# State-space mixer with heads on partitions: scan, broadcast loads and grouped matmul bursts in a two-layer decoder trunk

## The chip, the cores and the metric

The kernel runs on one core of a Trainium2 chip. The metric is device time in microseconds (us) of one execution. A profiled execution adds a trace of five engines: TensorE (PE, whose weight loads are listed as PEld), VectorE (DVE), ScalarE (ACT), GpSimd (POOL) and SyncE (SP), which issues the DMAs.

## The reference

The program is a decoder trunk of two layers on 256 positions of width 1024. Each layer normalises its input, runs three token mixers side by side (a state-space mixer, a retention, a gated linear attention), adds the gated sum back, and then runs a gated MLP with a short convolution over positions. The change lies in the state-space mixer alone. With `xs` (8 heads of 64), `bm` and `cm` (2 groups of 64 states, four heads to a group) and one raw step per head and position, it computes

```python
dt = softplus(dt_raw + ssm_dt_bias)            # (256, 8)
a = -exp(ssm_a_log)                            # (8,)
cum = cumsum(dt * a)                           # over positions, per head
decay[t, s] = exp(cum[t] - cum[s])             # s <= t, else 0
y[t] = sum over s <= t of (cm[t] . bm[s]) * decay[t, s] * (dt[s] * xs[s])
y = y + ssm_d * xs                             # then gated by silu(z) and group-normed
```

The sum is written in chunks in the reference; both kernels take all 256 positions at once, as two blocks of 128.

## The kernel before

All large products are float32 products in three terms: a weight is loaded in pieces of 128 x 1024 (`piece`, line 167), ACT rounds it to a high part `whi` (line 183), DVE takes the rest `wlo` (line 184), and PE multiplies high by high, high by low and low by high (lines 227 to 229 with 256 columns, lines 274 to 276 with 512). There are four buffers for raw pieces and six for split ones; each request for a piece issues the loads of up to five pieces ahead.

`stream` runs the main line of these products for one layer after the other. At each `yield` of the main line, every side task whose count has run out is advanced once (lines 1086 to 1090). One such step is one pass over a slice of a weight: six matmuls of 512 columns in `tok_major`, twelve of 256 in `chan_major`. The side task of the change is `ssm` (line 567): its `yield W[i]` puts so many steps between two of its parts. So the emission order is written out by hand, and from it the framework's planner lays down the order of each engine at build time, by its own estimates of when an instruction is ready. After that every engine runs in order.

In each layer `ssm` is spawned after `take_small` (line 923), which leaves the raw steps of the 8 heads on partitions 0 to 7 and, for a second part of the same product, on 64 to 71. Beside it the main line runs z, the first gates, rq, rk and rv; before the retention (`ret`) is spawned, `ssm` is finished (line 962). Its parts before the change are these.

- Lines 570 to 585: PE turns the raw steps to positions on partitions (`pick` adds the two parts), and DVE and ACT compute `dt` (softplus, through `log1p`) and `da` on tiles of 128 x 16.
- Lines 586 to 592: eight PE transposes bring `xs` to positions on partitions.
- Lines 593 to 599: three PE products with a triangle of ones and a block of ones make the running sum `ncum`.
- Lines 600 to 605: POOL makes `val = dt * xs` and scales `xs` by `ssm_d`.
- Lines 607 to 612: PE turns `ncum` back to heads on partitions, and it is split into two parts in `cum`.
- `decay` (line 615), four times, for two heads each: PE spreads a head's row of `cum` over 128 partitions (line 620), ACT adds the other position's sum (lines 624 and 626), POOL masks the upper triangle (line 629), ACT takes the exponential (line 631). The tiles have the tag `st` with two buffers.
- `score` (line 634), once for each group of states: products over 64 partitions, 0 to 63 for one group and 64 to 127 for the other. `masked` (line 641) multiplies scores into a decay tile on DVE.
- `scan_out` (line 548), four times: 12 products of scores with values, 24 rows in the trace.
- Lines 664 to 678: the sum is gated and normed, and `branch_operand` (line 534) transposes it on PE.

PSUM tiles of these parts come from a ring of four (`mx_tile`). The retention after it uses the same `scan_out`, and in its own `score` (lines 723 to 729) two heads on partitions 0 to 63 and 64 to 127 follow each other.

## Time and profile before

| | us |
|---|---|
| median of 3 runs | 927.43 (927.09 to 927.57) |
| the profiled execution | 928.57 |
| its span in the trace | 926.8 |

Engines' busy times, the waits of an engine and the matmul rows are read from that one execution. The start of a row is exact; matmuls overlap, so the time that a matmul takes from the engine is the distance from its start to the next one's start, not the length of its row.

### The profile page before, as it was taken

To read this page: it belongs to the slowest core of one execution; us is meant where nothing else is said; L and a number is where in the kernel's file an instruction comes from. 1 tells how busy PE (TensorE), PEld (TensorE's weight loads), DVE (VectorE), ACT (ScalarE), POOL (GpSimd) and SP (SyncE) were. 2 spreads that over 40 slices of the span, in tenths; PEclk is the share of its full clock that TensorE was granted. 3 is DMA by queue.
4 is the path that set the end of the run, shared out by engine and by line. 5 is a ranking of instruction groups with operands and counts; after the bars stand their busy time and mean duration, and the time that the engine had idled before them with its cause. 6 is when DMAs were issued, how large, how long until landed. Compare 5 with 4: busy or idle time off the path is not lost.

```text
span 926.8 us, 15382 instructions
## 1 busy us (share of the span) xinstructions
PE 908.8 (98%) x5918; PEld 805.8 (87%) x5918; DVE 711.5 (77%) x1111; ACT 506.2 (55%) x748; POOL 78.4 (8%) x74
## 2 busy tenths in 40 slices
PE   8999999999999999999999999999999999999995
PEld 7779888888889999999898897888888999999994
DVE  6976888576768887778799578877657797787775
ACT  6665454454456555555566645544445575555552
POOL 3022200003200000000002131000220000000001
PEclk9999999999999999999999999999999999999998
DMA  8774666456665655565456656544666565555631
GB/s 255 261 252 153 224 191 174 155 163 210 197 182 161 203 183 185 185 191 191 148 174 190 201 174 220 160 155 146 209 204 202 160 199 187 184 182 187 184 107 45
DMA packets 51289, 169.95 MB, mean 183 GB/s; under 512 B 5968, under 2 KB 8336, under 8 KB 51088
## 3 DMA queue, kind: packets, MB, share of 16 engines
q1 hardware_dynamic: 50928, 168.46, 57.3%
q8 instruction: 46, 0.75, 0.3%
q10 hardware_dynamic: 288, 0.52, 0.2%
q14 instruction: 27, 0.22, 0.1%
HBM read 165.81 MB, written 1.05 MB: 180 GB/s over the span
## 4 chain that ended last, share of the span: by engine, by line
PE 87%; DVE 4%; issue 3%; DMA 3%; ACT 2%; SPq 1%; POOL 0%; ACTq 0%; POOLq 0%; DVEq 0%
PE mm L227 12%; PE mm L228 12%; PE mm L229 12%; PE mm L274 11%; PE mm L276 11%; PE mm L275 11%; PE mx L1025 4%; PE mx L1026 4%; PE mx L1027 4%; DMA raw<-w_all 2%; DVE wlo L184 1%; PE mx L558 1%; PE mx L542 1%; SPq L704 1%; DMA x_t<-x_t 1%
## 5 line engine op out<-in xcount | busy, mean ns | idle before, releaser
L184 DVE TENSOR_TENSOR wlo<-raw,whi 128x1024 fp32r<-128x1024 f32 (+1 forms) x300 | 376.5, 1257 | 126.2 <-ACT whi L183 123.4
L183 ACT CAST whi<-raw 128x1024 fp32r<-128x1024 f32 (+1 forms) x302 | 311.6, 1034 | 270.0 <-PE mm L276 111.8
L227 PE MATMUL mm<-slot_h,whi 128*128 128x256 f32 x992 | 282.0, 285 | 1.6 <-ACT slot_h L302 1.6
L228 PE MATMUL mm<-slot_l,whi 128*128 128x256 f32 x992 | 281.0, 283 | 0.4 <-DVE slot_l L303 0.2
L229 PE MATMUL mm<-slot_h,wlo 128*128 128x256 f32 x992 | 281.0, 283 | 0.0
L274 PE MATMUL mm<-whi,slot_h 128*128 128x512 f32 x512 | 204.3, 399 | 0.9 <-DVE tm L459 0.9
L275 PE MATMUL mm<-wlo,slot_h 128*128 128x512 f32 x512 | 200.3, 391 | 0.3 <-DVE wlo L184 0.3
L276 PE MATMUL mm<-whi,slot_l 128*128 128x512 f32 x512 | 200.3, 391 | 0.0
L227 PEld LDWEIGHTS mm<-slot_h,whi 128*128 128x128 f32 x992 | 189.8, 191 | 4.9 <-ACT slot_h L302 2.2
L228 PEld LDWEIGHTS mm<-slot_l,whi 128*128 128x128 f32 x992 | 189.9, 192 | 2.8 <-DVE slot_l L303 1.0
L229 PEld LDWEIGHTS mm<-slot_h,wlo 128*128 128x128 f32 x992 | 189.9, 191 | 0.4 <-DVE wlo L184 0.2
L274 PEld LDWEIGHTS mm<-whi,slot_h 128*128 128x128 f32 x512 | 96.2, 188 | 22.1 <-DVE tm L459 1.4
L276 PEld LDWEIGHTS mm<-whi,slot_l 128*128 128x128 f32 x512 | 96.2, 188 | 20.2
L275 PEld LDWEIGHTS mm<-wlo,slot_h 128*128 128x128 f32 x512 | 96.3, 188 | 19.2 <-DVE wlo L184 0.7
L1015 DVE SCALAR_TENSOR_TENSOR tm<-tm,par 128x255 f32<-128x255 f32 (+1 forms) x176 | 73.6, 480 | 0.7 <-ACT tm L1013 0.7
L1025 PE MATMUL mx<-whi,slot_h 128*128 128x512 f32 x176 | 69.1, 392 | 0.0
L1026 PE MATMUL mx<-wlo,slot_h 128*128 128x512 f32 x176 | 69.0, 392 | 0.0
L1027 PE MATMUL mx<-whi,slot_l 128*128 128x512 f32 x176 | 68.5, 389 | 0.0
L1013 ACT ACTIVATE tm<-tm,par 128x256 f32<-128x256 f32 x88 | 48.0, 593 | 4.3 <-DVE tm L1008 4.3
L1008 DVE TENSOR_TENSOR tm<-mm,r_bc 128x512 f32<-128x512 f32 x44 | 30.4, 691 | 23.0 <-PE mm L229 23.0
L1019 ACT CAST slot_h<-tm 128x256 fp32r<-128x256 f32 x44 | 17.9, 406 | 49.1 <-DVE tm L1018 49.1
L1027 PEld LDWEIGHTS mx<-whi,slot_l 128*128 128x128 f32 x176 | 33.1, 188 | 7.2
(189 smaller groups left out, 727.7 us busy)
## 6 DMA issues: line engine op xcount, KB each, us to landing
raw<-w_all SPq DMA_DIRECT2D x292, 512.0 KB, 3.6
gate_b<-gate_b SPq DMA_DIRECT2D x12, 256.0 KB, 3.5
st<-ret_decay SPq DMA_DIRECT2D x8, 384.0 KB, 4.2
raw<-w_all SPq DMA_DIRECT2D x10, 256.0 KB, 4.1
x_t<-x_t SPq DMA_DIRECT2D x4, 256.0 KB, 5.7
xt<-x_tok SPq DMA_DIRECT2D x1, 1024.0 KB, 5.7
r_c<-q SPq DMA_DIRECT2D x16, 64.0 KB, 2.0
r_d<-q SPq DMA_DIRECT2D x16, 64.0 KB, 2.0
```

The costliest lines, as they stand in the source:

```text
L183: nc.scalar.copy(h_out, r_in)
L184: nc.vector.tensor_tensor(l_out, r_in, h_out.bitcast(F32), ALU.subtract)
L227: nc.tensor.matmul(o, lhsT=wh[:, c], rhs=ah[:, k, :], start=first, stop=False)
L228: nc.tensor.matmul(o, lhsT=wh[:, c], rhs=al[:, k, :], start=False, stop=False)
L229: nc.tensor.matmul(o, lhsT=wl[:, c], rhs=ah[:, k, :], start=False, stop=last)
L274: nc.tensor.matmul(acc[t], lhsT=ah[:, k, c], rhs=wh, start=first, stop=False)
L275: nc.tensor.matmul(acc[t], lhsT=ah[:, k, c], rhs=wl, start=False, stop=False)
L276: nc.tensor.matmul(acc[t], lhsT=al[:, k, c], rhs=wh, start=False, stop=last)
L1015: nc.vector.scalar_tensor_tensor(a[:, d:], u[:, :T - d], mx.pc("fconv_w", 3 * ct + 2 - d), a[:, d:], ALU.mult, ALU.add)
L1025: nc.tensor.matmul(o, lhsT=ah[:, a, tok], rhs=wh, start=first, stop=False)
L1026: nc.tensor.matmul(o, lhsT=ah[:, a, tok], rhs=wl, start=False, stop=False)
L1027: nc.tensor.matmul(o, lhsT=al[:, a, tok], rhs=wh, start=False, stop=last)
```

## The change

The raw steps stay with the heads on partitions: DVE adds the two parts, DVE and ACT compute `dt` on 8 x 256, and one DVE scan makes the running sum `cum`. It is written to a scratch tensor in DRAM, and for two heads at a time it is loaded back with each row spread over 128 partitions, as 256 and as 128 columns, straight into the decay tiles (`spread`). PE turns `dt` and `cum` together by two transposes. POOL masks the loaded tile first, and ACT then takes the exponential with the other position's sum as its bias, in four instructions for each decay tile. The scores of both groups are made at once, alternating between the groups, and `scan_out` comes in two bursts of two. The scaling of `xs` by `ssm_d` moves behind the first two decay tiles. The table of step counts `W` changes with it: the last `scan_out` is emitted 28 steps after the first advance of `ssm`, where it was 42. Bias and decay rate lie in the parameters as 8 x 1; two small selection tables are gone.

```diff
-W = (4, 5, 4, 4, 1, 6, 5, 3, 5, 3, 3, 4, 3, 2, 6, 2, 6, 2, 4, 5, 8)
+W = (7, 2, 2, 5, 3, 1, 4, 4, 3, 3, 4, 3, 2, 6, 2, 6, 2, 4, 5, 8)
...
+            bias, (ue, lq, rows) = self.pc("dt_bias")[:8], (t_mix() for _ in range(3))
+            rows = rows[:40, :T]
+            nc.gpsimd.memset(rows, 0.0)
+            u, e, q, dt, cum = ue[:8, :T], ue[:8, T:], lq[:8], rows[:8], rows[32:40]
+            nc.vector.tensor_tensor(u, small[:8], small[64:72], ALU.add)
+            nc.scalar.activation(e, u, AF.Abs, bias=bias)
+            nc.scalar.activation(e, e, AF.Exp, scale=-1.0)
+            log1p(e, q, dt)
+            nc.vector.tensor_scalar(u, u, bias, 0.0, ALU.add, ALU.max)
+            nc.vector.tensor_tensor(dt, dt, u, ALU.add)
+            nc.vector.tensor_scalar(u, dt, self.aneg, None, ALU.mult)
+            nc.vector.tensor_tensor_scan(cum, ones[:8], u, 0.0, ALU.mult, ALU.add)
             yield W[0]
-            pt = mx_tile()
-            for t in range(2):
-                nc.tensor.matmul(pt[:, 8 * t:8 * t + 8], lhsT=small[:, t * P:(t + 1) * P], rhs=pick,
-                                 start=(t == 0), stop=(t == 1))
...
+            there = dram.tile([8, T], F32, name="cum", tag="cum")
+            nc.sync.dma_start(there, cum)
+            def spread(h2):
+                dec = mix.tile([P, 2, 384], F32, name="dec", tag="st", bufs=2)
+                two_rows = there[2 * h2:2 * h2 + 2, :]
+                nc.sync.dma_start(dec[:, :, 0:256], two_rows.partition_broadcast(P))
+                nc.sync.dma_start(dec[:, :, 256:384], two_rows[:, P:].partition_broadcast(P))
+                return dec
+            yield W[1]
+            d0, d1 = spread(0), spread(1)
+            yield W[2]
...
-                yield W[1]
             pt = mx_tile()
-            nc.tensor.matmul(pt[:, 0:8], lhsT=tri, rhs=da[:, 0:8], start=True, stop=False)
-            nc.tensor.matmul(pt[:, 8:16], lhsT=ones[:, :P], rhs=da[:, 0:8], start=False, stop=False)
-            nc.tensor.matmul(pt[:, 8:16], lhsT=tri, rhs=da[:, 8:16], start=False, stop=True)
...
+            for t in range(2):
+                nc.tensor.transpose(pt[:, 40 * t:40 * t + 40], rows[:, t * P:(t + 1) * P], ident[:40, :40])
+            both = pt[:, :80].rearrange("p (t h) -> p t h", t=2)
+            dtT, ncum = (sm.tile([P, 2, 8], F32, name=n, tag=n, bufs=1) for n in ("dt", "nc"))
+            nc.vector.tensor_copy(dtT, both[:, :, :8])
+            nc.vector.tensor_scalar(ncum, both[:, :, 32:40], -1.0, None, ALU.mult)
...
-            yield W[2]
-            pt = mx_tile()
-            for t in range(2):
-                nc.tensor.transpose(pt[:40, t * P:(t + 1) * P], ncum[:, t, :], ident)
-            cum = slots[2][0][:40, 0, :]
-            nc.scalar.activation(cum, pt[:40, :T], AF.Copy, scale=-1.0)
-            nc.vector.scalar_tensor_tensor(cum[32:], pt[32:40, :T], -1.0, cum[32:].bitcast(F32), ALU.mult, ALU.subtract)
-            yield W[3]
-            def decay(h2):
-                dec = mix.tile([P, 2, 384], F32, name="dec", tag="st", bufs=2)
-                pb = mx_tile()
-                for j in range(2):
-                    h = 2 * h2 + j
-                    nc.tensor.matmul(pb[:, j * T:(j + 1) * T], lhsT=pick_r[:, h:h + 1].to_broadcast([40, P]), rhs=cum,
-                                     start=(j == 0), stop=(j == 1))
...
+            def decay(h2, dec):
                 for o in (0, 256):
                     nc.gpsimd.affine_select(dec[:, :, o:o + P], dec[:, :, o:o + P], pattern=[[0, 2], [1, P]],
                                             compare_op=ALU.is_ge, fill=NEG, base=0, channel_multiplier=-1)
-                nc.scalar.activation(dec, dec, AF.Exp)
-                return dec
...
+                for j in range(2):
+                    h = 2 * h2 + j
+                    nc.scalar.activation(dec[:, j, 0:256], dec[:, j, 0:256], AF.Exp, bias=ncum[:, 0, h:h + 1])
+                    nc.scalar.activation(dec[:, j, 256:384], dec[:, j, 256:384], AF.Exp, bias=ncum[:, 1, h:h + 1])
+            def scores():
+                pt = [mx_tile() for _ in range(2)]
+                for o, w, k in ((0, 256, 0), (256, 128, P)):
+                    for g in range(2):
+                        c = slice(64 * g, 64 * g + 64)
+                        nc.tensor.matmul(pt[g][:, o:o + w], lhsT=xbc[c, 4, k:k + P], rhs=xbc[c, 5, k:], start=(k == 0),
+                                         stop=(k > 0))
                 return pt
...
+            decay(0, d0)
+            decay(1, d1)
...
+            yield W[3]
+            sc = scores()
+            for d in (d0, d1):
+                masked(d, sc[0])
             yield W[4]
...
             py = [mx_tile() for _ in range(2)]
             self.scan_out(py, 0, d0, val)
+            self.scan_out(py, 1, d1, val)
+            yield W[5]
+            d2, d3 = spread(2), spread(3)
             yield W[6]
...
+            for h2, d in ((2, d2), (3, d3)):
+                decay(h2, d)
+                masked(d, sc[1])
             yield W[7]
             self.scan_out(py, 2, d2, val)
-            yield W[8]
             self.scan_out(py, 3, d3, val)
...
-            for o, p, n in ((pick_r, 32, 40), (pick, 64, P)):
-                nc.vector.tensor_tensor(o, ident[:n, :8], ident[:n, p:p + 8], ALU.add)
```

## Rows read from the trace of the kernel before

**Rows 1.** Page, busy time of each engine, share of span, instructions.
```profile
PE 908.8 (98%) x5918; PEld 805.8 (87%) x5918; DVE 711.5 (77%) x1111; ACT 506.2 (55%) x748; POOL 78.4 (8%) x74
```

**Rows 2.** Waits of PE, whole span: waiter, releaser, total us, times, longest.
```profile
PE mx L594 <- DVE da L585: 0.8, 1, 0.8
PE mx L542 <- DVE tx L563: 0.7, 2, 0.3
```

**Rows 3.** Windows, main-line matmuls (tile mm): stretch, length, PE busy (count), clock, DMA.
```profile
39.24:69.17 29.93, 26.66 (x109) 1.00 0.70 229
69.17:96.58 27.41, 23.80 (x193) 1.00 0.55 188
96.58:112.19 15.61, 13.73 (x59) 1.00 0.67 221
484.75:521.51 36.76, 34.57 (x144) 1.00 0.66 198
521.51:548.92 27.41, 23.80 (x193) 1.00 0.56 181
548.92:564.53 15.61, 13.76 (x59) 1.00 0.71 240
```

**Rows 4.** Timeline of PE, first layer: start, length, line, operation, tiles, shapes.
```profile
46.37 0.39 PE L274 MATMUL mm<-whi,slot_h 128*128 128x512 f32 x1
46.61 0.60 PE L590 MATMUL mx<-cs,xbc 128*128 128x128 f32 x4
...
47.51 0.40 PE L274 MATMUL mm<-whi,slot_h 128*128 128x512 f32 x1
...
55.25 0.39 PE L275 MATMUL mm<-wlo,slot_h 128*128 128x512 f32 x1
...
69.17 0.28 PE L227 MATMUL mm<-slot_h,whi 128*128 128x256 f32 x1
...
76.25 0.28 PE L229 MATMUL mm<-slot_h,wlo 128*128 128x256 f32 x1
76.46 0.92 PE L558 MATMUL mx<-sg_d,dec 128*64 128x64 f32 x24
77.30 0.50 PE L620 MATMUL mx<-slot_h,pick_r 40*128 40x256 f32 x2
```

**Rows 5.** Timeline of PE, around a lone scan_out and the retention's pair of scores.
```profile
99.10 0.39 PE L276 MATMUL mm<-whi,slot_l 128*128 128x512 f32 x1
...
100.83 0.40 PE L276 MATMUL mm<-whi,slot_l 128*128 128x512 f32 x1
...
115.41 0.39 PE L276 MATMUL mm<-whi,slot_l 128*128 128x512 f32 x1
115.73 0.71 PE L727 MATMUL mx<-r_c,r_d 64*128 64x256 f32 x4
...
117.16 0.40 PE L276 MATMUL mm<-whi,slot_l 128*128 128x512 f32 x1
```

**Rows 6.** Timeline of DVE, first layer: small steps of the state-space chain.
```profile
45.85 0.17 DVE L578 TENSOR_TENSOR u<-mx,par 128x16 f32<-128x16 f32 x1
...
48.80 0.17 DVE L298 SCALAR_TENSOR_TENSOR dt<-lq,e 128x16 f32<-128x16 f32 x1
...
55.39 1.08 DVE L585 TENSOR_TENSOR da<-dt,aneg 128x8 f32<-128x8 f32 x2
...
59.67 0.42 DVE L612 SCALAR_TENSOR_TENSOR slot_h<-mx,slot_h 8x256 fp32r<-8x256 f32 x1 [0.21 <-ACT slot_h L611]
```

**Rows 7.** DMA issues: tiles, queue, count, KB each, median us to landing.
```profile
st<-ret_decay SPq DMA_DIRECT2D x8, 384.0 KB, 4.2
...
r_c<-q SPq DMA_DIRECT2D x16, 64.0 KB, 2.0
```

**Rows 8.** Waits of ACT's weight casts, 40 to 115 us.
```profile
ACT whi L183 <- PE mm L228: 9.0, 6, 2.9
...
ACT whi L183 <- DMA raw<-w_all: 1.9, 2, 1.7
```

More of the change, by code (lines that the diff above doesn't have):

```diff
@@ L134, in hybrid_trunk @@
     tmp = ctx.enter_context(tc.tile_pool(name="tmp", bufs=4))
+    dram = ctx.enter_context(tc.tile_pool(name="dram", bufs=1, space=bass.MemoryType.DRAM))
     sm = ctx.enter_context(tc.tile_pool(name="sm", bufs=2))
@@ L143, in hybrid_trunk @@
     rst = cs[:, CO_RST:CO_RST + T]
-    tri = cs[:, CO_TRI:CO_TRI + P]
-    pick_r = cpool.tile([40, 8], F32R, name="pick_r")
-    pick = cpool.tile([P, 8], F32, name="pick")
     ones = cpool.tile([P, T], F32, name="ones")
@@ L439, in __init__ @@
                                     ALU.mult)
-            self.aneg = sm.tile([P, 8], F32, name="aneg", tag="aneg")
-            nc.scalar.activation(self.aneg, self.pc("a_log", 0, 8), AF.Exp)
+            self.aneg = sm.tile([8, 1], F32, name="aneg", tag="aneg")
+            nc.scalar.activation(self.aneg, self.pc("a_log")[:8], AF.Exp)
             nc.vector.tensor_scalar(self.aneg, self.aneg, -1.0, None, ALU.mult)
@@ L568, in ssm @@
             xbc, rh, small = self.xbc, self.norm.rh, self.small
-            yield W[0]
-            pt = mx_tile()
-            for t in range(2):
-                nc.tensor.matmul(pt[:, 8 * t:8 * t + 8], lhsT=small[:, t * P:(t + 1) * P], rhs=pick,
-                                 start=(t == 0), stop=(t == 1))
-            u, e, dt, da = (sm.tile([P, 16], F32, name=q, tag=q, bufs=1) for q in ("u", "e", "dt", "da"))
-            ncum = sm.tile([P, 2, 40], F32, name="nc", tag="nc", bufs=1)
-            nc.gpsimd.memset(ncum, 0.0)
@@ L577, in ssm @@
-            lq = sm.tile([P, 32], F32, name="lq", tag="lq", bufs=1)
-            nc.vector.tensor_tensor(u.rearrange("p (t h) -> p t h", t=2), pt[:, :16].rearrange("p (t h) -> p t h", t=2),
-                                    self.pc("dt_bias", 0, 8).unsqueeze(1).to_broadcast([P, 2, 8]), ALU.add)
-            nc.scalar.activation(e, u, AF.Abs)
-            nc.scalar.activation(e, e, AF.Exp, scale=-1.0)
-            log1p(e, lq, dt)
-            nc.vector.scalar_tensor_tensor(dt, u, 0.0, dt, ALU.max, ALU.add)
@@ L630, in decay @@
                                             compare_op=ALU.is_ge, fill=NEG, base=0, channel_multiplier=-1)
-                nc.scalar.activation(dec, dec, AF.Exp)
-                return dec
-            def score(g):
-                c = slice(64 * g, 64 * g + 64)
-                pt = mx_tile()
-                nc.tensor.matmul(pt[:, 0:256], lhsT=xbc[c, 4, 0:P], rhs=xbc[c, 5, :], start=True, stop=False)
-                nc.tensor.matmul(pt[:, 256:384], lhsT=xbc[c, 4, P:T], rhs=xbc[c, 5, P:T], start=False, stop=True)
+                for j in range(2):
[9 more added lines that the diff above has]
+                                         stop=(k > 0))
                 return pt
@@ L642, in masked @@
                 nc.vector.tensor_tensor(dec, dec, sc[:, :384].unsqueeze(1).to_broadcast([P, 2, 384]), ALU.mult)
-            d0 = decay(0)
-            yield W[4]
-            sc = score(0)
-            masked(d0, sc)
-            d1 = decay(1)
-            yield W[5]
-            masked(d1, sc)
+            decay(0, d0)
+            decay(1, d1)
+            for t in range(2):
+                x3 = xs[:, t, :].rearrange("p (h d) -> p h d", h=8)
+                nc.gpsimd.tensor_tensor(x3, x3, self.pc("ssm_d", 0, 8).unsqueeze(2).to_broadcast([P, 8, 64]),
+                                        ALU.mult)
+            yield W[3]
+            sc = scores()
+            for d in (d0, d1):
+                masked(d, sc[0])
+            yield W[4]
             py = [mx_tile() for _ in range(2)]
             self.scan_out(py, 0, d0, val)
-            d2 = decay(2)
+            self.scan_out(py, 1, d1, val)
+            yield W[5]
+            d2, d3 = spread(2), spread(3)
             yield W[6]
-            self.scan_out(py, 1, d1, val)
-            sc = score(1)
-            masked(d2, sc)
-            d3 = decay(3)
+            for h2, d in ((2, d2), (3, d3)):
+                decay(h2, d)
+                masked(d, sc[1])
             yield W[7]
-            masked(d3, sc)
             self.scan_out(py, 2, d2, val)
-            yield W[8]
             self.scan_out(py, 3, d3, val)
@@ L1155, in _lay_params @@
         put(l, "fconv_b", cols(i["ffn_conv_b"][l]))
-        for name, key in (("dt_bias", "ssm_dt_bias"), ("a_log", "ssm_a_log"), ("ssm_d", "ssm_d")):
-            put(l, name, np.broadcast_to(i[key][l].reshape(1, 8), (P, 8)))
+        put(l, "dt_bias", i["ssm_dt_bias"][l].reshape(8, 1))
+        put(l, "a_log", i["ssm_a_log"][l].reshape(8, 1))
+        put(l, "ssm_d", np.broadcast_to(i["ssm_d"][l].reshape(1, 8), (P, 8)))
     return par
```

45 lines of the change are left out of this document (16 added, 29 removed).

## The prediction

> **What bounds the kernel now.** I read the page's busy times first: PE is busy for 98% of the span, DVE for 77%, ACT for 55% [rows 1]. The waits of PE come next: in the part that changes it waited only for the running sum's operand, 0.8 us in one layer, and for the normed rows ahead of `branch_operand`, 0.7 us in two layers [rows 2]. So the time is the sum of what is fed to PE, and an instruction taken from PE is worth its time in full as long as PE isn't made to wait. What the state-space work costs PE I read from windows over the main line's matmuls [rows 3] and from the starts in the timeline [rows 4].
>
> A main-line matmul of 512 columns takes 0.2276 us: from the start at 47.51 to that at 55.25 lie 34 of them. One of 256 columns takes 0.120 us: 59 from 69.17 to 76.25 [rows 4]. Three stretches hold the state-space work of a layer; a stretch less its main-line matmuls at these rates is the cost of everything put between them, waits included. Of the counts in rows 3 one each is a matmul begun ahead of the stretch, and in the third stretch of each layer another lies on its edge. First layer: 29.93 - 108 x 0.2276 = 5.35; 27.41 - 192 x 0.120 = 4.37; 15.61 - 57 x 0.2276 = 2.64; together 12.36 us. Second layer: 36.76 - 143 x 0.2276 = 4.21; 4.37; 2.64; together 11.22. Both layers: 23.58 us [rows 3].
>
> **The change part by part.** *Work left on PE.* Priced by rows in the same way, for one layer:
> - Four transposes cost 47.51 - 46.37 less three main-line matmuls (0.68), 0.46 us [rows 4]. The eight for `xs` and the eight of `branch_operand` stay: 4 x 0.46 = 1.84.
> - The two transposes of `rows` have no row. Between nothing (they ride in a burst already paid for) and half of four, I take 0.23, because they need an operand that the others don't and can be laid apart.
> - A lone `scan_out` costs 100.83 - 99.10 - 0.68 = 1.05 [rows 5]; one with more behind it, from its start at 76.46 to the next burst's at 77.30, costs 0.84 [rows 4]. So entering and leaving a burst is 0.2 us. Two bursts of two: 2 x (1.05 + 0.84) = 3.78.
> - The alternating scores stand nearest to the retention's pair, which also lies on partitions 0 to 63 and 64 to 127: 117.16 - 115.41 - 0.68 = 1.07 for both [rows 5]. If the groups didn't overlap, it would be up to twice that.
>
> The sum is 1.84 + 0.23 + 3.78 + 1.07 = 6.92 a layer, 13.84 for two. PE is spared 23.58 - 13.84 = 9.74 us: the eight spreading products, the selection and triangle products, the way back to heads, some seven entries into a burst, and the waits of rows 2, since `ssm` ends 14 steps earlier and its tail no longer meets the last part of rk. In the bounds: if the scores cost twice 1.07 and both double bursts are laid apart, 2 x (1.07 + 0.4) = 2.9 less; if the transposes of `rows` are free, 0.5 more.
>
> *The chain on 8 partitions.* A step on 128 x 16 takes 0.17 us on DVE, one on 8 x 256 takes 0.42 [rows 6]. Nine DVE steps at 0.42 (add, four of `log1p`, three, and the scan, which no row shows and which I price like the others; twice that at the worst) for eight at 0.17 are 2.4 us more, and if ACT's six steps grow by the same 0.25, 1.5 more. The chain before ran from 45.85 to 56.47, 10.6 us, with weight work between its steps [rows 6]; now some 14.5. It is covered: a step of the main line is six matmuls, 1.37 us, or twelve of 256, 1.44; the store waits 7 steps, the transposes of `rows` 11. What hides it is main-line work, and what is late next if it fails is PE at those transposes. ACT gives back more than it takes (four exponentials of 768 and sixteen additions go, sixteen exponentials come), and the parameters, the two dropped tables and a memset on POOL are off the path: nothing.
>
> *The Trainium skill speaks against this step: "Trainium Kernel Development and Optimization", Best Practices, wants every tile on 128 partitions. By that rule a step that uses 8 of them wastes the engine; the rows say 0.25 us a step, and the sum would lose that only if PE waited for the chain. No run here yet shows whether it does.*
>
> *The round trip by DMA.* The trace of before has no such load. The store is 8 KB; the smallest data DMA with a row, 64 KB, lands after 2.0 us [rows 7], which I take. A spread is 384 KB, as is a load of `ret_decay`, which lands after 4.2 [rows 7]. For two spreads in a row the near end is 4.2 and 2.2 more (the 4.2 less the 2.0 of a small one), 6.4 us. The far end goes by pieces: 64 KB in rows of 1 KB took 2.0 us, and 768 KB at that rate take 24. I take the near end, since size and target are those of the `ret_decay` row and many loads fly at once. *The skill's "DMA: Bandwidth & Descriptors", Why small descriptors are slow, gives a fixed 3 cycles for each packet beside one for every 32 bytes; an estimate by it is 19% more for 512 B and 9% for 1 KB, so 7.3 us for the pair at the most. No run here shows it yet.*
>
> On SP the store waits for the scan, and the second pair of spreads waits until the first burst of `scan_out` frees its two buffers; behind them on the queue are raw pieces, gate biases and rotary copies. That is free as long as split weights lie ahead: ACT's casts waited 9.0 us for PE to give back buffers in one group alone and only 1.9 us for raw pieces [rows 8]. If that cover is gone, each us is one of PE. From the second pair's issue to its burst there are 1 + 4 + 4 = 9 steps, 12.6 us. Two landings (6.4) and eight exponentials in turn (8 x 0.42, 3.4, by the row of the same width) leave 2.8. The first pair has 2 + 5 + 3 = 10 steps, 13.8.
>
> *New waits.* The planner goes by its estimates, and the one such miss on PE in this part was 0.8 us [rows 2]. I allow 0.8 us in all for its miss on loads that it can't see in company.
>
> **The rivals.**
> - *Spreads land late, in part.* At 11.5 us for a pair, PE waits 11.5 + 3.4 - 12.6 = 2.3 at the second burst and 1.1 at the first, 3.4 a layer: 927.43 - 9.74 + 6.8 = 924.5. For it: rows of 512 B and 1 KB, beside a weight stream. Against it: the 4.2 us of rows 7.
> - *The DMA round trip takes PE's place as the bound (slower).* The same place, further out: both bursts of each layer stand behind their loads. Kernel and change break even where the two waits of a layer come to 4.9 us, and it is slower by 0.2% from 5.8 us, that is from 12.7 us for a pair. At 14 us: 4.8 + 3.6 = 8.4 a layer, 927.43 - 9.74 + 16.8 = 934.5. The far end of 24 us speaks for it; that one small copy's rate is mostly its fixed time speaks against it.
> - *The chain is late.* On 8 lanes it is 3.9 us longer; where DVE is full, in the first layer, PE waits for all of that at the transposes of `rows`: 918.5 + 3.9 = 922.4. The 0.8 us wait of rows 2 is of this kind, at the same place. This is the rival by the rule on 128 partitions.
> - *The change doesn't do what it says.* The groups don't overlap and the bursts come apart: 2.9 us less gain, 921.4. It lies inside the forecast's range.
>
> **How the numbers follow.** The sum against the profiled execution: 928.57 - 9.74 + 0.8 = 919.6. That execution lies 1.14 above the median of 927.43, and its span of 926.8 leaves 1.8 around it that doesn't change. So the median is forecast at 919.6 - 1.1 = 918.5. Chances: forecast, with the last rival in it, 0.59 (916 to 922); spreads late in part 0.17 (922 to 927, a fifth of it within 0.2%); chain late 0.08; slower 0.12; no net change for a reason not seen 0.04. A measurement of this kernel can tell about 0.2%, 1.9 us, from no change. Faster: 0.59 + 0.14 + 0.08 = 0.81; same 0.03 + 0.04 = 0.07; slower 0.12. The low end has free transposes and no new wait, 918.5 - 0.5 - 0.8 = 917.2, with some 1.5 below it for the miss of rates read to 0.001 us over 700 matmuls and for waits that vanish; the high end takes in spreads late in part. 915.7 to 926.2 leaves out the slower case and little else.
>
> **What would show it.** Right: the same three stretches of a layer cost some 6.9 us over their main-line matmuls, `scan_out` comes in two bursts of 48 rows, the scores of both groups in about 0.9 us, and PE's list of waits has nothing over 1 us that names a decay tile or a load. The first pair of spreads lands within 7 us. Wrong: waits of PE at `scan_out` whose releaser is the mask on DVE, with a late spread behind it; a wait at the transposes of `rows` for the scan; or casts that wait for raw pieces behind a blocked SP. A time above 925.5 would say that the loads are not covered.

## The result, and the profile after

| | before | changed |
|---|---|---|
| median, us | 927.45 (927.09 to 927.57, 4 runs) | 934.88 (934.55 to 935.47, 4 runs) |
| the profiled execution, us | 928.57 | 934.77 |
| its span, us | 926.8 | 933.0 |

The changed kernel is slower: ratio 1.0075, 95% interval 1.0058 to 1.0091. The forecast was 918.5, with a range of 915.7 to 926.2.

The busy line of the page of the changed kernel: engine, busy us, share of the span, instructions.

```profile
PE 906.3 (97%) x5882; PEld 805.0 (86%) x5882; DVE 717.2 (77%) x1109; ACT 503.9 (54%) x738; POOL 78.1 (8%) x74
```

Against [rows 1] PE has 36 instructions and 2.5 us of busy time less, and its span is 6.2 us longer. So the work did leave PE, and something else came in. The list of PE's waits in the changed kernel (waiter, releaser, total us, times, longest) names it:

```profile
PE mx L554 <- DVE dec L632: 7.6, 3, 3.9
PE mx L538 <- DVE tx L559: 3.6, 2, 1.8
...
PE mx L602 <- DVE tx L577: 0.3, 1, 0.3
```

Before there were 1.5 us of such waits [rows 2]; now `scan_out` (L554) waits for its masked decay tile (L632), `branch_operand` (L538) for the normed rows (L559), and the transposes of `rows` (L602) hardly wait. Where this stands in time, by PE's timeline of the changed kernel, scores and both bursts of the first layer, first burst of the second (start, length, line, operation, tiles, shapes, wait before it):

```profile
53.77 0.92 PE L627 MATMUL mx<-xbc 64*128 64x256 f32 x8
...
60.90 0.39 PE L270 MATMUL mm<-whi,slot_h 128*128 128x512 f32 x1
65.14 1.55 PE L554 MATMUL mx<-sg_d,dec 128*64 128x64 f32 x24 [3.85 <-DVE dec L632]
66.62 0.80 PE L271 MATMUL mm<-wlo,slot_h 128*128 128x512 f32 x1
67.34 1.55 PE L554 MATMUL mx<-sg_d,dec 128*64 128x64 f32 x24
68.82 0.80 PE L272 MATMUL mm<-whi,slot_l 128*128 128x512 f32 x1
69.42 0.63 PE L270 MATMUL mm<-whi,slot_h 128*128 128x512 f32 x1
...
70.62 0.40 PE L270 MATMUL mm<-whi,slot_h 128*128 128x512 f32 x1
...
79.89 1.62 PE L554 MATMUL mx<-sg_d,dec 128*64 128x64 f32 x48
...
515.33 0.39 PE L272 MATMUL mm<-whi,slot_l 128*128 128x512 f32 x1
518.11 1.55 PE L554 MATMUL mx<-sg_d,dec 128*64 128x64 f32 x24 [2.39 <-DVE dec L632]
521.05 1.55 PE L554 MATMUL mx<-sg_d,dec 128*64 128x64 f32 x24 [1.39 <-DVE dec L632]
```

The second burst is the planned one, 48 rows in 1.62 us. The first comes 4.2 us (first layer) and 2.8 us (second) after the matmul ahead of it, in two pieces with main-line work or a second wait between them, and it is slow as well: 24 rows take 1.55 us. Windows of the changed kernel show why (stretch, length, busy time and count of PE, PEld, DVE, ACT, POOL, then PE's granted clock, DMA share, GB/s):

```profile
60.00:64.50 4.50, 1.29 (x6) 0.75 (x4) 2.62 (x3) 1.95 (x6) 3.66 (x5) 0.91 0.91 284
64.50:70.00 5.50, 4.86 (x52) 4.00 (x53) 3.99 (x4) 3.44 (x6) 0.00 (x0) 0.50 0.57 215
70.00:74.00 4.00, 4.00 (x18) 3.30 (x17) 1.35 (x2) 2.44 (x5) 1.54 (x3) 0.93 0.55 150
...
518.00:524.00 6.00, 4.50 (x52) 3.91 (x53) 2.17 (x3) 2.02 (x4) 0.71 (x2) 0.50 0.46 152
```

After PE had idled 3.85 us in the first layer, and 2.39 us in the second, the granted clock stood at 0.50, the 1.2 GHz level, for some 5.5 to 6 us.

An account of it: for every burst, the distance from the main-line matmul ahead of it to the first one behind it from which on the main line is back at its rate, less the main-line matmuls in between at 0.2276 or 0.120 us. For the first layer's first burst these are the starts at 60.90 and 70.62 with six matmuls in between: 9.72 - 6 x 0.2276 = 8.35. This is the measure that the prediction used over whole stretches [rows 3]. (The expectations below go by a shorter count, to the second matmul behind a burst; it puts the two layers at 15.97 and 14.9 us, and the half clock in both at some 4.1.)

| changed kernel, us over the main line | first layer | second layer | forecast each |
|---|---|---|---|
| transposes of xs | 1.60 | 0.88 | 0.92 |
| transposes of `rows` | 0.46 | 0.84 | 0.23 |
| scores | 1.06 | 1.06 | 1.07 |
| first double burst | 8.35 | 7.99 | 1.89 |
| second double burst | 1.74 | 1.74 | 1.89 |
| transposes of `branch_operand` | 2.85 | 2.84 | 0.92 |
| sum | 16.06 | 15.35 | 6.92 |

Together 31.4 us where the kernel before had 23.6: 7.8 more, by which the profiled execution should take 928.57 + 7.8 = 936.4; it took 934.77, and the 1.6 us between them are not explained. Of the 17.6 us between 31.4 and the forecast of 13.8, the first bursts carry 12.6 and the tails 3.85. In the first layer's 8.35 the wait is 3.85; two bursts laid apart cost 2 x 1.05 at full clock [rows 5]; what is left, 2.4, is the half clock. In the second layer it is 7.99 - 3.78 - 1.89 = 2.3.

**The path to the first burst.** The timeline of DVE in the changed kernel, first layer, has the first and the last step of the chain on 8 partitions:

```profile
39.58 0.41 DVE L570 TENSOR_TENSOR tx<-small 8x256 f32<-8x256 f32 x1
...
51.45 0.68 DVE L577 TENSOR_TENSOR_SCAN tx<-ones,tx 8x256 f32<-8x256 f32 x1
```

The timeline of SP has the store (L581) and the first spread (L587) of each layer:

```profile
52.20 0.35 SPq L581 DMA_DIRECT2D cum<-tx  x1
...
54.88 0.38 SPq L587 DMA_DIRECT2D dec<-cum  x1
...
505.96 0.30 SPq L581 DMA_DIRECT2D cum<-tx  x1
...
509.84 0.38 SPq L587 DMA_DIRECT2D dec<-cum  x1
```

The timeline of POOL has the product for `val` (L609), that with `ssm_d` (L638) and the masks (L614), first and second layer:

```profile
54.76 3.95 POOL L609 TENSOR_TENSOR sg_d<-sg_c,dt 128x512 f32<-128x512 f32 x2 [35.08 <-DVE nc L606]
58.67 3.03 POOL L638 TENSOR_TENSOR sg_c<-sg_c,par 128x512 f32<-128x512 f32 x2
61.66 1.22 POOL L614 TENSOR_SCALAR_AFFINE_SELECT dec<-dec 128x256 f32<-128x256 f32 x2
63.51 0.78 POOL L614 TENSOR_SCALAR_AFFINE_SELECT dec<-dec 128x256 f32<-128x256 f32 x2 [0.63 <-DMA dec<-cum]
...
507.37 2.05 POOL L609 TENSOR_TENSOR sg_d<-sg_c,dt 128x512 f32<-128x512 f32 x2 [251.38 <-DVE nc L606]
...
514.26 0.41 POOL L614 TENSOR_SCALAR_AFFINE_SELECT dec<-dec 128x256 f32<-128x256 f32 x1 [1.85 <-DMA dec<-cum]
...
518.42 0.41 POOL L614 TENSOR_SCALAR_AFFINE_SELECT dec<-dec 128x256 f32<-128x256 f32 x1 [1.76 <-DMA dec<-cum]
```

Second layer: the chain runs from 492.53 to 505.88 (13.3 us); the first spread is issued 3.9 us after the store; the last mask that waited for a load starts 8.6 us after that, at 518.42; DVE has multiplied the scores into the second tile (L632) at 520.99. That is 28.5 us from the first step. When DVE took up that step, PE had 515.33 - 492.53 = 22.8 us of other work ahead of the burst. In the first layer it had 60.90 - 39.58 = 21.3, and the same path took until 66.48, 26.9 us; there POOL had its product with `ssm_d` (L638) in front of the masks until 61.66. Part of that is POOL's own lateness: the two instructions of L609 took 3.95 us there, beside two weight steps of DVE (L180, 54.60 to 57.80), and 2.05 in the second layer, where DVE was idle for most of them.

### The profile page after: what moved, and what is told of

Same layout as the page of the kernel before. It is cut to its first block, busy times and chain, and to the rows that moved or that the text cites. A ratio compares the mean times of both kernels' runs of the same rounds, so it can differ in the third digit from the quotient of the medians.

```text
span 933.0 us, 15326 instructions
## 1 busy us (share of the span) xinstructions
PE 906.3 (97%) x5882; PEld 805.0 (86%) x5882; DVE 717.2 (77%) x1109; ACT 503.9 (54%) x738; POOL 78.1 (8%) x74
## 3 DMA queue, kind: packets, MB, share of 16 engines
HBM read 168.94 MB, written 1.06 MB: 182 GB/s over the span
## 5 line engine op out<-in xcount | busy, mean ns | idle before, releaser
L180 DVE TENSOR_TENSOR wlo<-raw,whi 128x1024 fp32r<-128x1024 f32 (+1 forms) x300 | 375.1, 1252 | 125.6 <-ACT whi L179 122.7
L270 PEld LDWEIGHTS mm<-whi,slot_h 128*128 128x128 f32 x512 | 96.7, 189 | 21.3 <-issue 0.7
```

Of the source, the lines that this page charges most:

```text
L180: nc.vector.tensor_tensor(l_out, r_in, h_out.bitcast(F32), ALU.subtract)
L270: nc.tensor.matmul(acc[t], lhsT=ah[:, k, c], rhs=wh, start=first, stop=False)
```

## The experiments

The theory after this reading: the raw steps reach the first burst by one path in series (chain, store, spreads, masks, exponentials, products), which is 5 to 6 us longer than the work that PE has meanwhile. Its rivals: the spreads as such are slow; the chain on 8 partitions alone is at fault; POOL's order is at fault. A second theory is for the tail. The same account by burst for the kernels that changed it, with the time that it forecasts, 928.57 + sum - 23.58 (only bursts of the state-space mixer are counted):

| us | first burst, layers 1, 2 | second | tail, layers 1, 2 | sum of both layers | by the account | profiled execution |
|---|---|---|---|---|---|---|
| changed kernel | 8.35, 7.99 | 1.74, 1.74 | 2.85, 2.84 | 31.4 | 936.4 | 934.77 |
| e1_burst_later | 1.82, 1.74 | 6.19, 1.85 | 3.68, 6.58 | 27.3 | 932.3 | 930.81 |
| e4_no_store | 2.72, 1.75 | 1.73, 1.74 | 5.91, 4.13 | 24.6 | 929.6 | 928.09 |
| e5_short_chain | 8.42, 3.49 | 1.74, 1.74 | 2.83, 2.83 | 28.6 | 933.6 | 933.65 |
| e8_counts | 3.20, 1.75 | 1.74, 1.74 | 1.54, 1.92 | 17.3 | 922.3 | 923.08 |
| e9_rotary_dve | 7.47, 8.33 | 1.74, 1.74 | 1.47, 1.16 | 27.4 | 932.3 | 931.91 |
| e10_counts_rotary | 3.20, 1.75 | 1.74, 1.74 | 5.15, 3.60 | 22.9 | 927.9 | 926.93 |
| e11_pe_first_pair | 7.07, 3.19 | 1.73, 1.73 | 4.36, 3.08 | 28.5 | 933.5 | 932.74 |
| e12_all | 2.85, 1.76 | 1.75, 1.74 | 2.69, 0.91 | 17.2 | 922.2 | 921.36 |
| e13_scale_dve | 4.04, 4.68 | 1.74, 1.73 | 5.81, 2.83 | 27.3 | 932.3 | 930.82 |

It holds within 1.7 us in every row, so what is read below from bursts is what moved the time of that one execution. The executions of one kernel lie up to 7 us apart here, and the profiled one can be at an end: in e1 and e11 it is the fastest of four, by 2.9 and 2.4 us. All ratios are against the kernel before, on the same chip. The diffs are against the changed kernel.

### Is it the distance alone?

**e1_burst_later**: the first burst five steps later.

```diff
-W = (7, 2, 2, 5, 3, 1, 4, 4, 3, 3, ...
+W = (7, 2, 2, 5, 8, 1, 4, 4, 3, 3, ...
```

> The first burst of scan products is emitted five main-line steps later (the fifth count 3 to 8), and all of the state-space part behind it with it. Theory 1 (the path from the raw steps through the chain, the store and the first pair of loads is longer than its cover, so PE waits at the first burst, and TensorE then runs at its lower clock for some us): the burst comes 20 matmuls of 0.228 us later, 4.6 us, which is more than the waits of 3.9 and 3.8 us; the 7.6 us of waits in two layers go, and with them some 4.1 us of slow clock: 934.9 - 11.7 = 923.2. Rival (the loads are held up by the weight stream and by blocked queues, and are as late again): waits of 3 us or more stay, 932 or more.

Measured: 934.0 (930.81 to 935.2), ratio 1.0074 (1.0055 to 1.0094). The first bursts are what the theory said, 1.82 and 1.74 with no wait, but the time is not: 934.0 where 923.2 was expected. PE's waits in e1_burst_later:

```profile
PE mx L538 <- DVE tx L559: 6.3, 2, 3.9
PE mx L554 <- DVE dec L632: 2.7, 1, 2.7
```

The second pair's spreads wait for the first burst to free its buffers, so they moved five steps with it, and the counts behind them stayed: the second burst of the first layer waits 2.7 us and both tails wait longer than before (2.4 and 3.9 us against 1.8). One distance was mended and the next two were too short.

**e7_tail_later**: the transposes of `branch_operand` five steps later.

```diff
-W = (7, 2, 2, 5, 3, 1, 4, 4, 3, 3, ...
+W = (7, 2, 2, 5, 3, 1, 4, 4, 8, 3, ...
```

> The transposes of the normed rows are emitted five steps later (count 3 to 8), nothing else moves. In the changed kernel PE waits there for 1.8 us in each layer, where it was 0.3 before, since small DVE steps of the norm (128 x 4) take 0.8 and 1.25 us beside POOL's rotary sums in place of 0.16. Theory 2 (this is a second, separate loss, and it is one of order): the 3.6 us go, and with a burst of eight in place of 2 and 6 some more: 931 to 932. Rival (the rotary sums move along, or the next work waits as long): 934.5 or more.

Measured: 935.46, ratio 1.0086 (1.007 to 1.0102). In the first layer the planner put the first of these transposes behind the same main-line matmul in both kernels, the 454th of the program, and in the second it did so too; the waits there were 2.0 and 1.8 us. The edit didn't move what it was to move, so it says nothing.

**e8_counts**: all three distances.

```diff
-W = (7, 2, 2, 5, 3, 1, 4, 4, 3, 3, ...
+W = (7, 2, 2, 5, 7, 1, 4, 5, 13, 3, ...
```

> Step counts alone are changed: 7, 2, 2, 5, 7, 1, 4, 5, 13 in place of 7, 2, 2, 5, 3, 1, 4, 4, 3. The first burst comes 14 matmuls of 512 columns (3.2 us) later, and the transposes of the normed rows come some 16 us behind the second burst, where it was 12.2. Theory 1 and 2 together (two losses of order: the first burst ahead of its loads, the transposes ahead of the norm's small steps, each with slow clock behind it): no wait over 1 us on PE in this part, granted clock at 1.0, some 7.3 us a layer for the state-space work: 934.9 less (15.97 - 7.4) and (14.9 - 7.2), 918.6. Rival (a wait that goes comes back later, as in the run with the first burst alone moved): 928 or more.

Measured: 922.96 (922.65 to 923.85), ratio 0.9953 (0.9938 to 0.9968), faster than both kernels. PE's waits in e8_counts that belong to the state-space mixer:

```profile
PE mx L554 <- DVE dec L632: 1.2, 2, 0.7
...
PE mx L538 <- DVE tx L559: 0.9, 3, 0.3
```

No operation differs from the changed kernel, only where three of them are emitted, and 11.9 us of 934.88 go. It is 4.4 us above the expectation. That put 7.4 and 7.2 us for the two layers, and the account has 9.1 and 8.2: the first layer's first burst is 1.3 us longer (the two waits), and the tails are 0.6 and 1.0 us above their 0.92. The other 1.7 us have no place among the bursts. So the distance is what the changed kernel lacked; the operations are worth about what was forecast for them.

**e2_fill**: does a fill of 52 useless matmuls ahead of the first burst cost what it takes less the waits? They write a PSUM tile that the burst then overwrites.

```diff
+            xh = slots[0][0]
+            for _ in range(52):
+                nc.tensor.matmul(py[0][:, 0:T], lhsT=xh[:, 0, 0:P], rhs=xh[:, 0, :], start=True, stop=True)
             self.scan_out(py, 0, d0, val)
             self.scan_out(py, 1, d1, val)
```

> 52 useless matmuls of 256 columns (0.12 us each, 6.2 us) on PE ahead of the first burst in each layer, which fill the time in which PE waits there (3.9 us, and 2.3 more since the burst now comes 10 main-line matmuls earlier). They overwrite nothing that is used. The time at which the masked tiles are ready stays. Theory 1 with the clock as part of its price: granted clock stays at 1.0 behind the burst, and the 4.1 us of slow clock go although the wait's time is all spent: 934.9 - 4.1 = 930.8. Rival (the slow clock costs nothing, the wait is all): 934.9 or some more.

Measured: 941.37, ratio 1.0148 (1.0132 to 1.0163). The fill takes 6.24 us a layer, and the granted clock is 1.00 from 62 to 68 us. The waits at the first bursts shrink to one of 0.4 us, and with the fill these bursts cost 8.64 and 7.97 us, 16.6 together where wait and half clock had made 16.3. So the fill cost what it took away: in the second layer 6.24 us stand where 3.8 us of wait and 2.3 of half clock stood. But the kernel is 6.5 us slower, and that lies in the first layer, away from the first burst. Its tail went from 2.85 to 7.65, by a wait of 4.0 us (1.8 before) and by half clock behind it: the granted clock was 0.50 from 99.5 to 105 us. The second burst took 0.6 us more and the transposes of xs, which come ahead of the fill, 0.8 more. Why the tail came later is not shown. The tail's 2.6 us show once more what a long wait costs beyond its length.

### Which part of the path?

**e4_no_store**: the loads read rows of the `ret_decay` table, which is there from the start, and `ncum` is multiplied by 0 so that the exponentials see the table alone. The decay by the running sum is left out of the result.

```diff
-                two_rows = there[2 * h2:2 * h2 + 2, :]
+                two_rows = dret[0, 2 * h2:2 * h2 + 2, 0:T]
...
-            nc.vector.tensor_scalar(ncum, both[:, :, 32:40], -1.0, None, ALU.mult)
+            nc.vector.tensor_scalar(ncum, both[:, :, 32:40], 0.0, None, ALU.mult)
```

> The loads read a table of constants in DRAM of the same shape in place of the stored sums, so they wait neither for the chain nor for the store; the added sum is multiplied by zero. What is computed differs from the reference; every instruction stays. The planner puts the burst 8 matmuls (1.8 us) earlier. Theory 1 (it is the path through chain and store that makes the loads late): the loads are issued some 5 us or more earlier, PE's waits at the first burst are under 1 us a layer, the clock stays: 923 to 925. Rival (the loads themselves are slow, rows of 512 B and 1 KB beside the weights): waits of 3.8 + 1.8 us a layer stay: 935 to 938.

Measured: 926.93 (924.9 to 931.42, 10 runs), ratio 0.9993 (0.9975 to 1.0012). Loads of the same shape that don't stand behind chain and store leave 2.72 and 1.75 at the first bursts, and the only wait there is 0.5 us for POOL's L638. The loads take no less time to land (medians of 4.9 and 5.6 us against 4.3 and 4.9), but the first layer's first pair was issued between 28.5 and 35.5 us, and its masks were done by 41.9. So it is being behind the chain and the store that makes the spreads late, and not their length alone. The edit also took the masks out from behind L638, so it doesn't part the loads from POOL's order. The tails got worse (5.91 and 4.13), as in e1.

**e5_short_chain**: two of the four rounds of `log1p` left out in the state-space mixer, so `dt` is wrong by that much.

```diff
-            log1p(e, q, dt)
+            log1p(e, q, dt, LOG1P[2:])
...
-    def log1p(e, q, p):
+    def log1p(e, q, p, poly=LOG1P):
...
-        for i, (_, m) in enumerate(LOG1P):
+        for i, (_, m) in enumerate(poly):
```

> Two of the four rounds of the logarithm are left out in the state-space chain (its result is then not the reference's): the chain is some 3.0 us shorter by the distance of its rounds (1.5 us each). Theory 1 (the first burst's wait is the sum of everything from the raw steps on): the store and the loads come 3 us earlier, waits of 3.9 and 3.8 fall to some 1 to 1.6 us, and the slow clock behind them shrinks: 927 to 930. Rival (the loads land when the weight stream lets them, whatever the chain): waits as before, 934.9.

Measured: 933.68 (930.95 to 934.86), ratio 1.0063 (1.0045 to 1.008). PE's timeline of e5_short_chain, second layer:

```profile
517.51 0.92 PE L554 MATMUL mx<-sg_d,dec 128*64 128x64 f32 x24
519.80 0.92 PE L554 MATMUL mx<-sg_d,dec 128*64 128x64 f32 x24 [1.37 <-DVE dec L632]
```

In the second layer the chain took 11.5 us instead of 13.3, the wait fell from 3.8 to 1.4 and the clock stayed up (0.92 for 24 rows): the chain is part of the path. In the first layer the chain took 10.6 us instead of 12.5, but DVE took up its first step 1.3 us later, so the scan ended only 0.6 us earlier; the first spread was issued 4.5 us after the store instead of 2.7, and the burst stayed at 8.42. The timeline of POOL there:

```profile
61.38 2.85 POOL L614 TENSOR_SCALAR_AFFINE_SELECT dec<-dec 128x256 f32<-128x256 f32 x4
```

All four masks run in a row behind L638 (58.32 to 61.35) without a wait for a load, so in this layer POOL was last. Neither theory gave that split.

**e11_pe_first_pair**: for the first pair PE spreads `cum` again, as in the kernel before; store and loads remain for the second pair. (`pick_r` is the selection table of the kernel before, made again; those two lines are left out here.)

```diff
-            d0, d1 = spread(0), spread(1)
+            ch = slots[2][0][:40, 0, :]
+            nc.scalar.activation(ch, rows, AF.Copy)
+            nc.scalar.activation(ch[:8], cum, AF.Copy)
+            nc.vector.tensor_tensor(ch[32:], cum, ch[32:].bitcast(F32), ALU.subtract)
...
-            decay(0, d0)
-            decay(1, d1)
+            d0, d1 = (mix.tile([P, 2, 384], F32, name="dec", tag="st", bufs=2) for _ in range(2))
+            for h2, dec in ((0, d0), (1, d1)):
+                pb = mx_tile()
+                for j in range(2):
+                    h = 2 * h2 + j
+                    nc.tensor.matmul(pb[:, j * T:(j + 1) * T], lhsT=pick_r[:, h:h + 1].to_broadcast([40, P]), rhs=ch,
+                                     start=(j == 0), stop=(j == 1))
+                for j in range(2):
+                    nc.scalar.copy(dec[:, j, 0:256], pb[:, j * T:(j + 1) * T])
+                    nc.vector.tensor_copy(dec[:, j, 256:384], pb[:, j * T + P:(j + 1) * T])
+                decay(h2, dec)
```

> The changed kernel, but for the first pair of decay tiles PE spreads cum again, by products with a selection (as the kernel before did); store and loads stay for the second pair, the chain on 8 partitions stays. Adds four products of 256 columns a layer, some 1 us of PE each layer. Theory (the round trip through DRAM is one part of one long path from the raw steps to the first burst): in the second layer, where POOL's masks waited for loads until 518.4, the wait of 3.8 us and the half clock after it go, 5.7 us; in the first, where POOL's scaling ends at 61.7, some 2 us: 934.9 - 7.7 + 2 = 929. Rival (the chain on 8 partitions alone makes the burst late, the loads only happen to end last): the waits stay at 2 us or more in both layers and the products are added, 934 to 937.

Measured: 935.55 (932.74 to 936.18), ratio 1.0074 (1.0055 to 1.0092). The timeline of POOL in the second layer of e11_pe_first_pair (its L651, L618 and L555 are L638, L614 and L554 of the changed kernel):

```profile
511.41 3.04 POOL L651 TENSOR_TENSOR sg_c<-sg_c,par 128x512 f32<-128x512 f32 x2
514.41 2.47 POOL L618 TENSOR_SCALAR_AFFINE_SELECT dec<-dec 128x256 f32<-128x256 f32 x4
```

And that of PE:

```profile
518.74 0.92 PE L555 MATMUL mx<-sg_d,dec 128*64 128x64 f32 x24 [0.67 <-DVE dec L636]
520.14 0.92 PE L555 MATMUL mx<-sg_d,dec 128*64 128x64 f32 x24 [0.48 <-DVE dec L636]
```

There POOL's masks no longer wait for loads, the wait falls from 3.8 to 1.15 and the half clock goes: the round trip is part of the path too. In the first layer the wait hardly moved (3.5 us), because POOL reached the masks at 61.89, behind its L651, as it did at 61.66. The account gives 2.9 us less than the changed kernel, and the profiled execution had 2.0 less, but the median of the four runs is not lower. So the time supports the rival's number, the second layer's rows the theory; the forecast of 929 missed POOL's place in the first layer.

**e3_pool_order** emits the scaling by `ssm_d` behind the first burst.

```diff
             decay(0, d0)
             decay(1, d1)
-            for t in range(2):
-                x3 = xs[:, t, :].rearrange("p (h d) -> p h d", h=8)
-                nc.gpsimd.tensor_tensor(x3, x3, self.pc("ssm_d", 0, 8).unsqueeze(2).to_broadcast([P, 8, 64]),
-                                        ALU.mult)
...
             d2, d3 = spread(2), spread(3)
+            for t in range(2):
+                x3 = xs[:, t, :].rearrange("p (h d) -> p h d", h=8)
+                nc.gpsimd.tensor_tensor(x3, x3, self.pc("ssm_d", 0, 8).unsqueeze(2).to_broadcast([P, 8, 64]),
+                                        ALU.mult)
```

> The scaling of xs by ssm_d on POOL (3.0 us in two instructions) is emitted behind the first burst. In the changed kernel it stands ahead of the first masks on POOL; in the first layer the masks start when it ends (61.7), in the second it ended at 512.4 and the mask waited for its load until 514.3. Theory 3 (POOL's order is part of the first layer's wait): the first layer's wait falls by some 2 us, the second's stays: 931.5 to 933. Rival (the first layer's loads are late as well): 934.9.

Measured: 935.1, ratio 1.0081 (1.0064 to 1.0098). The planner still put the product on POOL at 59.61, ahead of the first masks at 62.6: the emission order alone didn't move it. Inconclusive. **e13_scale_dve** moves it to DVE instead.

```diff
-                nc.gpsimd.tensor_tensor(x3, x3, self.pc("ssm_d", 0, 8).unsqueeze(2).to_broadcast([P, 8, 64]),
+                nc.vector.tensor_tensor(x3, x3, self.pc("ssm_d", 0, 8).unsqueeze(2).to_broadcast([P, 8, 64]),
```

> The changed kernel with the scaling of xs by ssm_d on DVE instead of POOL, nothing else. In the first layer POOL began the first masks only when the scaling was done, at 61.7 us; in the second it waited for loads. If POOL's order holds up the first layer's first burst, its wait of 3.9 us falls by 1.5 to 3 us and the second layer's stays at 3.8: 931 to 933.5. Rival: the loads land no sooner than the scaling ended, or DVE comes later by what it took over: 934.5 or more.

Measured: 930.65 (928.24 to 934.23, 10 runs), ratio 1.003 (1.0016 to 1.0044). The timeline of POOL in the first layer of e13_scale_dve:

```profile
58.53 0.69 POOL L614 TENSOR_SCALAR_AFFINE_SELECT dec<-dec 128x256 f32<-128x256 f32 x1
61.13 0.41 POOL L614 TENSOR_SCALAR_AFFINE_SELECT dec<-dec 128x256 f32<-128x256 f32 x1 [1.91 <-DMA dec<-cum]
```

And that of PE:

```profile
63.37 0.92 PE L554 MATMUL mx<-sg_d,dec 128*64 128x64 f32 x24 [1.86 <-DVE dec L632]
```

The first mask comes 3.1 us earlier, then POOL waits for loads; PE's wait falls from 3.85 to 1.86 and the clock stays up. So in the first layer POOL's order and the loads are late side by side, the loads by about 2 us less. The second layer's first burst also fell, to 4.68 (waits of 2.6 in two), which I hadn't expected. The tail of the first layer went from 2.85 to 5.81.

### The tail

The timeline of DVE in the first layer of the changed kernel, at the small steps of `rsqrt`:

```profile
88.18 0.16 DVE L281 TENSOR_SCALAR rs_y<-rs_v 128x4 int32<-128x4 int32 x1
88.85 0.81 DVE L283 TENSOR_TENSOR rs_a<-rs_y 128x4 f32<-128x4 f32 x1
90.24 1.21 DVE L180 TENSOR_TENSOR wlo<-raw,whi 128x1024 fp32r<-128x1024 f32 x1
91.38 1.25 DVE L285 SCALAR_TENSOR_TENSOR rs_y<-rs_a,rs_y 128x4 f32<-128x4 f32 x1
92.66 0.16 DVE L283 TENSOR_TENSOR rs_a<-rs_y 128x4 f32<-128x4 f32 x1
```

The timeline of POOL beside it, at the rotary sums:

```profile
88.34 1.29 POOL L693 TENSOR_TENSOR q<-q,s 128x512 f32<-128x512 f32 x1 [12.30 <-DVE rs_y L281]
90.33 2.28 POOL L693 TENSOR_TENSOR q<-q,s 128x512 f32<-128x512 f32 x1 [0.70 <-DVE rs_a L284]
```

A step of 0.16 us ends when POOL's instruction ends: L283 at 89.66 (POOL 89.63), L285 at 92.63 (POOL 92.61). And POOL's second sum takes 2.28 instead of 1.29 where DVE's L180 was under way as it began. The Trainium skill says this in "SBUF — State Buffer", SBUF: two separate sides: GpSimd and a DVE instruction with two SBUF inputs share a pair of ports, which one of them holds for a whole instruction. These rows agree with it. **e9_rotary_dve** puts the rotary sums of L693 on DVE.

```diff
-                nc.gpsimd.tensor_tensor(q, q, s, (ALU.subtract, ALU.add)[f])
+                nc.vector.tensor_tensor(q, q, s, (ALU.subtract, ALU.add)[f])
```

> POOL's rotary sums go to DVE, all else stays. Theory 2 (the norm's small DVE steps on 128 x 4 take 0.8 and 1.25 us because POOL works beside them): they fall to 0.16, the wait at the transposes falls from 1.8 to under 0.5 us a layer; the first burst's waits stay. 934.9 - 2.6 to 3.9: 931.0 to 932.3. Rival (DVE is simply full there, and the added sums of 0.68 us make it fuller): waits of 2 us or more, 935 or more.

Measured: 932.37 (931.25 to 933.76), ratio 1.0054 (1.0039 to 1.0069). All these small steps take 0.15 to 0.17 us, the tails fall to 1.47 and 1.16, the waits there from 3.6 to 0.5 in all, and the first bursts' waits stay (7.9 us in three). So the second theory's mechanism holds, but not all of the 2.5 us is its: the planner also put the transposes seven main-line matmuls later in each layer, 0.84 us, which is 1.7 of the 3.1 us by which the waits fell. The rest, some 1.4 us, is the rows that were ready sooner.

**e10_counts_rotary** joins the edits of e8 and e9, **e12_all** those of e8, e9 and e13.

> The changed kernel with both repairs that helped alone: the counts that start the two bursts four and one steps later and the tail five steps later (alone 922.96), and POOL's rotary sums on DVE (alone 932.4 against 934.9). If the tail's remaining waits at the transposes of branch_operand (0.3 and 0.6 us) come from POOL beside DVE's small steps, they go: 921.5 to 922.5. Rival: the later counts had already moved the tail out of POOL's way, so that the rotary sums on DVE bring nothing or cost it time: 923.0 to 924.0.

> As e10_counts_rotary, and the scaling of xs by ssm_d on DVE instead of POOL. In the first layer the scaling of 3.0 us stands on POOL ahead of the first masks, and the first burst still waited 1.2 us in two waits with the later counts. If POOL's order is what that burst waits for, the wait goes: 1 us under e10_counts_rotary, 920.5 to 921.5. Rival: the loads or the two exponentials in turn set that burst, or DVE's added 2 us delay its masks: no less than e10_counts_rotary.

Measured, with 27 runs of the kernel before between them: e10 925.63 (923.52 to 928.42, 12 runs), ratio 0.9967 (0.9955 to 0.9979); e12 923.04 (921.0 to 927.77, 10 runs), ratio 0.9944 (0.9925 to 0.9963). e10 falls to its rival and beyond: its tails are 5.15 and 3.60. With the counts of e8 the tail meets the rotary work on DVE: five of the small steps, 0.16 us each, came every 0.67 us with a rotary instruction between them, and in the first layer the grouped products behind them started 21.3 us after the second burst, against 18.2 in e8. e12 is below e10 by more than expected (their intervals just overlap), but not at the place that was expected: the first layer's first burst moved only from 3.20 to 2.85, the tails to 2.69 and 0.91. e8 and e12 can't be told apart by their intervals; either beats both kernels.

## Why the prediction was wrong, point by point

- *PE's own work: right.* Cases without a wait, from e8, e12 and the changed kernel, are 1.10 for the transposes of xs in two groups (0.88 where they come together), 0.46 for those of `rows`, 1.06 for the scores, 1.74 and 1.74 for the bursts, 0.91 for the tail: 7.0 us in the first layer, and 7.2 in the second, where `rows` have 0.85 with a wait of 0.3 in it. Forecast 6.92. The saving by these is 23.58 - 14.2 = 9.4 us; the forecast was 9.74. The scores took what the retention's pair takes, so the rival that the change doesn't do what it says is out.
- *The chain: right in size.* Forecast 14.5 us, measured 12.5 and 13.3; the scan took 0.68 where 0.42 was put, the other steps 0.33 to 0.41. PE waited 0.3 us for it at the transposes of `rows`, not the 3.9 of the chain rival. So the rule of the Trainium skill that the rival stood beside ("Trainium Kernel Development and Optimization", Best Practices) cost PE nothing at that place; the longer steps went into the path behind.
- *The failing step: the covers.* The prediction set "the store waits 7 steps, the transposes of `rows` 11" against the chain, and "the first pair has 2 + 5 + 3 = 10 steps, 13.8" against the spreads. But a spread can't be issued before the store has landed, and the store not before the scan has ended; the chain that outran its 7 steps took its excess from the 10. The right sum is one path against all 19 steps up to the burst, 19 x 1.37 = 26.0 us. Its own terms, 14.5 + 2.0 + 6.4 + 3.4 = 26.3, would have shown that nothing was left. Of the 26.0, 21.3 and 22.8 were left when DVE took up the first step behind its convolution work, and the path took 26.9 and 28.5. In the first layer POOL's products, for which the sum has no term, were last on that path, until 61.66; e13, which takes one of them off POOL, brought the wait there from 3.85 to 1.86.
- *The round trip: half as much again.* 2.0 + 6.4 = 8.4 was put; measured in the second layer 3.9 + 8.6 = 12.5. The page of the changed kernel has, for each load, the time to landing:

```profile
st<-ret_decay SPq DMA_DIRECT2D x8, 384.0 KB, 5.2
...
dec<-cum SPq DMA_DIRECT2D x8, 256.0 KB, 4.3
...
dec<-cum SPq DMA_DIRECT2D x8, 128.0 KB, 4.9
```

  A load of its own is near the 4.2 of [rows 7]; four of them behind each other end late. The DMA share was 0.87 to 0.91 while they were in flight, which I take for the reason; no run shows it. The sum with the packet cost of the Trainium skill's "DMA: Bandwidth & Descriptors", Why small descriptors are slow, an estimate of 7.3 us a pair (7.6 with the 19% of 512 B on all of it), was short as well: the pair took 8.6.
- *The price of a wait: left out.* A wait was priced at its length. Here the wait at each first burst was followed by 5 us or so at the granted clock of 0.50, which cost 2.4 and 2.3 us more; in e13 (first layer, a wait of 1.86), e5 and e11 (second layer, 1.37 and 0.67) the rows behind it ran at full clock, 24 in 0.92 us, and nothing but the wait was lost.
- *That the waits of rows 2 go: wrong.* The tail did leave rk's last part, and met POOL's rotary sums instead; 0.7 us became 3.6. The row that warned was in [rows 6]: L585 took 1.08 us for two steps on 128 x 8, from 55.39, while POOL's product L602 ran from 54.42 to 57.38.
- *The slower rival* had the effect (a wait behind the mask on DVE, with a late spread behind it) and by chance the time, 934.5. Its mechanism was off: it asked for 14 us a pair and for both bursts; the pair took 8.6, and the second burst, whose 9 steps begin with its own loads, never waited in the changed kernel.

## What to carry to other kernels

Add up a side task as one path, from the instant at which its first operand is really taken up to its first use on the busy engine, and set that sum against all the work in between; covers that are counted link by link hide what one link hands on to the next. When work leaves the engine that sets the time, the distances written out by hand must be measured anew and moved together: here three step counts were worth 12 us, and one alone (e1) was worth nothing that shows. Before a small step on DVE is called cheap, look at what POOL runs at that moment.

## What the runs showed of the hardware that was not expected

- A row of small DVE steps with two inputs, 0.15 to 0.17 us each, had members of 0.81 and 1.25 us that ended with a POOL instruction; POOL's own went from 1.29 to 2.28.
- Between the issue of an 8 KB store to DRAM and that of the first load that depends on it lay 2.7 and 3.9 us in the changed kernel, 1.6 in e13 and 4.5 in e5 (first layers); a spread took 3.5 to 7.6 us to land in the changed kernel, medians 4.3 (256 KB) and 4.9 (128 KB).
- Behind a wait of 2.74 us (e1, second burst of the first layer) 24 rows still took 0.92 us; only the main-line matmuls behind them, from 84.31 to 87.62, were 0.21 us apart instead of 0.12, at a granted clock of 0.50. Behind the wait of 2.39 us in the changed kernel the rows themselves took 1.55 us.
- A scan of 256 elements on 8 partitions took 0.68 us, a scalar_tensor_tensor of the same shape 0.41.
